# Second norm of a hybrid transformer block: four row blocks of the first gate unit multiplied before the root is known, the root applied in PSUM, five weight blocks split ahead

## The chip, the cores and the metric

The kernel runs on one core of one Trainium2 chip. Its metric is the device time of one execution in microseconds (us). Three runs of the kernel before took 2433.78, 2435.13 and 2435.26 us; their median is 2435.13 us. Engines are named as in the profile: PE multiplies matrices, PEld loads its weights, DVE and ACT do elementwise work, POOL and SP mostly issue transfers (DMAs).

## The reference, cut to what matters

One layer of a generator over 512 latent tokens of width 2048: two groups of recurrent heads, an output projection with a residual, and a SwiGLU feed-forward with a 3x3 depthwise convolution on its gate branch. All data are float32. The change lies between the output projection and the feed-forward:

```python
def rmsnorm(x, g):
    y = x * rsqrt(mean(square(x), axis=-1) + EPS)
    return y * g
...
x = x + gt1 * merge_groups(...)                  # einsum with w_out
h2 = rmsnorm(x, g_norm2) * (1 + sc2) + sh2       # the second norm
u = einsum('btd,df->btf', h2, w_up)
u_gate, u_val = split(u, 2)
g = conv3x3(u_gate) + conv_b
x = x + gt2 * ((silu(g) * u_val) @ w_down)
```

The root `rsqrt(...)` is one number per token, the scale `g_norm2 * (1 + sc2)` and the shift `sh2` are one number per row of the width. So `W^T h2` is the root times `W^T (scale * x)`, plus `W^T shift`, for all rows or for some of them.

## The kernel before, in words

Activations lie transposed: a row block is 128 of the 2048 rows of the width on the partitions, and 512 tokens along the free dimension. There are 16 row blocks (`KT`), taken in 8 pairs (`KP`). Every large product is done three times with the operands split in a high and a low part (`mm3`: high by high, low by high, high by low). ACT makes the high part by a cast (`hi_...`), DVE the low part by a subtraction (`lo_...`). The helper `mm` records every product at line 113, so the trace is read by the names of the tiles.

The output projection (`wo`) runs as four units, `n` = 0 to 3. Each unit makes four row blocks of the result in four PSUM accumulators and goes through eight weight blocks of 512 KB (`raw_wo`, split into `hi_wo` and `lo_wo`, two buffers each). After a unit, DVE adds the residual (`residual`, L1210, `x<-wo,mod,x`), POOL stores the row block to DRAM, ACT squares it (`square`, L1220), and DVE adds the squares into one tile, `sqsq` (L102), except the last two, which stay apart. During the projection DVE also works off the modulation vectors (`raw_m<-raw_m,crow`, L332, with loads of 512 KB), which give `modc[3]` (shift) and `modc[4]` (scale) for the second norm.

Then comes the second norm. `token_rstd` sums the squares over the partitions by products with a column of ones (`ps_rms`), ACT and DVE make the root (`mean_rsqrt`, L176 to L181, on four columns), and a second set of products spreads the root over the partitions (`rb_rms`). Three and seven further products, whose results nobody reads, stand before and after those (`idle_products`, named `rb_rms<-sqsq,cst` and `idle<-sqsq,cst` in the trace).

With the root, three instructions make one normed row block: DVE multiplies by scale and root (L1290, `x<-x,mod,rb_rms`), ACT adds the shift into the high part (L1291, `bqh`), DVE makes the low part (L1292, `bql`). The first gate unit (`ug`, `up_gate(0)`, 384 columns in three accumulators) multiplies all 16 row blocks in eight steps with weight blocks of 384 KB, and the first value unit (`uv`) does the same with its own weights. At the same time DVE and ACT make sums of row blocks (`token_sums`, tiles `bth`, `btl`), which the later units need: these take 512 columns with seven products for each two by two of blocks (`seven`). The convolution of the first unit (`cv`, L1384) runs on DVE during the value unit and the second gate unit, and its result (`gh`, `gl`) is what the first down unit (`dn`) multiplies with the weights `hi_d`, `lo_d`.

The order on each engine comes from a scheduler that follows the program's order and moves forward what stands under `tc.high_priority()`. Where `pinned` is set, PE keeps the program's order: it does so from the last output unit to the end of the norm. An engine executes its list strictly in order. Loads of weights go through SP's queue, in order too. A new tile pool takes the memory of a closed one and waits for its last readers.

## Time and profile before

| what | us |
|---|---|
| median of three runs | 2435.13 |
| the profiled execution | 2434.19 |
| its span, first to last instruction | 2432.0 |
| PE busy in the span | 2406.7 (99%) |
| DVE busy | 1801.9 (74%) |
| ACT busy | 1015.7 (42%) |
| last output unit's products end, about | 1063.6 |
| products of the first gate unit begin | 1071.65 |
| products of the first value unit begin | 1104.58 |
| first product of the second gate unit | 1137.22 |
| first product of the first down unit | 1177.37 |

Times within the execution are counted from the start of the span. A row of the timeline gives the start, the length, the engine, the line, the operation and, where they are equal and follow each other, their number; in square brackets stands how long the engine had been idle before it and what ended that. Instructions of one engine overlap a little, so that the distance of two starts, not the length, is what one costs in a row of equal ones. A row of the table by stretches of time gives the busy time of PE, PEld, DVE, ACT and POOL with the number of instructions, then the granted clock of PE, the busy share of the DMA engines and GB/s.

### The profile page before, as it was taken

The numbers are of one execution on the slowest core, as the hardware profiler recorded it, in microseconds if no ns is written. First come the engines' busy times: TensorE is split into PE (matmuls) and PEld (weight loads), VectorE is DVE, ScalarE is ACT, GpSimd is POOL, SyncE is SP. The second block draws the span as 40 slices with busy tenths as digits, with TensorE's granted clock in tenths as the row PEclk, the third lists the DMA queues.
The fourth block names the chain that finished last, engine by engine and source line by source line (L and its number), as shares of the span: only waits on it lengthen the run. The fifth ranks groups of instructions, "written<-read, shape, count | busy, mean of one in ns | idle before, by whom it ended". The sixth has DMA issues, their size and how long they took to land.

```text
span 2432.0 us, 38493 instructions
## 1 busy us (share of the span) xinstructions
PE 2406.7 (99%) x15334; PEld 2167.3 (89%) x15334; DVE 1801.9 (74%) x2880; ACT 1015.7 (42%) x1508; POOL 179.6 (7%) x227
## 2 busy tenths in 40 slices
PE   8999999999999999999999999999999999999998
PEld 5888899899988888888898989898989999999997
DVE  6777856645556576779987887878787878787886
ACT  5235533322223232256544444544444444444445
POOL 0000000000000000000202010101010111111022
PEclk9999999999999999999999999999999999999999
DMA  9951111233355798833646464645555555546464
GB/s 386 332 176 44 46 53 53 81 128 114 122 199 198 230 331 273 288 115 113 156 119 161 117 154 116 157 113 144 134 131 142 134 140 123 147 124 153 114 184 137
DMA packets 120902, 375.73 MB, mean 154 GB/s; under 512 B 13976, under 2 KB 14994, under 8 KB 120722
## 3 DMA queue, kind: packets, MB, share of 16 engines
q1 hardware_dynamic: 93634, 318.46, 39.3%
q0 software_dynamic: 26656, 54.03, 12.1%
q8 instruction: 120, 1.97, 0.3%
q10 hardware_dynamic: 432, 0.79, 0.1%
q14 instruction: 60, 0.49, 0.1%
HBM read 322.87 MB, written 50.35 MB: 153 GB/s over the span
## 4 chain that ended last, share of the span: by engine, by line
PE 92%; DVE 4%; DMA 2%; ACT 1%; issue 1%; SPq 0%; DVEq 0%
PE a L113 18%; PE uv L113 18%; PE ug L113 18%; PE dn L113 17%; PE ga L113 7%; PE wo L113 7%; PE po L113 2%; DVE cv L1384 1%; PE sl L113 1%; PE ps_m L113 1%; DMA raw_m<-in_w_mod 1%; PE st L113 1%; DMA raw_uv<-in_w_up 1%; PE cst L113 1%; DVE lo_d L108 0%
## 5 line engine op out<-in xcount | busy, mean ns | idle before, releaser
L113 PE MATMUL dn<-gh,lo_d 128*128 128x512 f32 x672 | 262.5, 391 | 1.1 <-DVE lo_d L108 1.1
L113 PE MATMUL dn<-gh,hi_d 128*128 128x512 f32 x672 | 261.8, 390 | 0.0
L113 PE MATMUL dn<-gl,hi_d 128*128 128x512 f32 x672 | 261.7, 389 | 0.0
L1384 DVE SCALAR_TENSOR_TENSOR cv<-pads,cwt,cv 128x512 f32<-128x512 f32 x344 | 238.9, 745 | 0.6
L1438 POOL DMA_DIRECT2D x2d<-st x160 | 140.2, 927 | 1141.5 <-ACT st L1437 1059.9
L108 DVE TENSOR_TENSOR lo_buv<-sum_uv,hi_buv 128x1024 fp32r<-128x1024 f32 x80 | 98.0, 1225 | 103.4 <-ACT hi_buv L107 103.3
L332 DVE SCALAR_TENSOR_TENSOR raw_m<-raw_m,crow 128x1024 f32<-128x1024 f32 x128 | 154.5, 1228 | 1.2 <-DMA raw_m<-in_w_mod 1.2
L113 PEld LDWEIGHTS dn<-gh,lo_d 128*128 128x128 f32 x672 | 126.1, 188 | 29.8 <-DVE lo_d L108 3.8
L113 PE MATMUL a<-hi_h,hTh 128*128 128x256 f32 x512 | 151.7, 296 | 0.5 <-ACT e L450 0.5
L113 PEld LDWEIGHTS dn<-gl,hi_d 128*128 128x128 f32 x672 | 126.2, 188 | 26.0
L113 PEld LDWEIGHTS dn<-gh,hi_d 128*128 128x128 f32 x672 | 126.2, 188 | 25.7
L113 PE MATMUL a<-lo_h,hTh 128*128 128x256 f32 x512 | 144.7, 283 | 0.0
L113 PE MATMUL a<-hi_h,hTl 128*128 128x256 f32 x512 | 144.7, 283 | 0.0
L107 ACT CAST hi_d<-raw_d 128x1024 fp32r<-128x1024 f32 x86 | 88.6, 1031 | 132.6 <-PE ug L113 70.6
L108 DVE TENSOR_TENSOR lo_d<-raw_d,hi_d 128x1024 fp32r<-128x1024 f32 x86 | 102.8, 1195 | 47.9 <-ACT hi_d L107 47.2
L113 PE MATMUL ug<-bth,hi_bug 128*128 128x256 f32 x480 | 136.8, 285 | 0.2 <-DVE t L1403 0.2
L113 PE MATMUL uv<-bql,hi_auv 128*128 128x256 f32 x480 | 135.9, 283 | 0.0
L113 PE MATMUL uv<-bqh,lo_auv 128*128 128x256 f32 x480 | 135.9, 283 | 0.0
L113 PE MATMUL uv<-bth,hi_buv 128*128 128x256 f32 x480 | 135.9, 283 | 0.0
L113 PE MATMUL uv<-btl,hi_buv 128*128 128x256 f32 x480 | 135.9, 283 | 0.0
L113 PE MATMUL uv<-bth,lo_buv 128*128 128x256 f32 x480 | 135.9, 283 | 0.0
L113 PE MATMUL ug<-bqh,lo_aug 128*128 128x256 f32 x480 | 135.9, 283 | 0.0
(432 smaller groups left out, 7267.4 us busy)
## 6 DMA issues: line engine op xcount, KB each, us to landing
raw_m<-in_w_mod SPq DMA_DIRECT2D x184, 512.0 KB, 5.0
raw_d<-in_w_down SPq DMA_DIRECT2D x82, 512.0 KB, 3.5
raw_ug<-in_w_up SPq DMA_DIRECT2D x80, 512.0 KB, 3.5
x2d<-st POOLq DMA_DIRECT2D x160, 256.0 KB, 5.4
raw_uv<-in_w_up SPq DMA_DIRECT2D x80, 512.0 KB, 5.0
raw_h<-in_w_heads SPq DMA_DIRECT2D x64, 512.0 KB, 3.5
raw_ga<-in_w_gates SPq DMA_DIRECT2D x32, 512.0 KB, 3.6
raw_wo<-in_w_out SPq DMA_DIRECT2D x32, 512.0 KB, 4.8
```

The costliest lines, as they stand in the source:

```text
L107: cast[0] = S.copy(hi, x).ins
L108: return V.tensor_tensor(out=lo, in0=x, in1=hi.bitcast(F32), op=ALU.subtract).ins
L113: ins = PE.matmul(*args, **kw)
L332: V.scalar_tensor_tensor(out=x, in0=x, scalar=1.0, in1=crow[0], op0=ALU.mult, op1=ALU.mult, accum_out=mtot[:, at : at + 1])
L1384: V.scalar_tensor_tensor(out=t3, in0=src, scalar=w, in1=t3, op0=ALU.mult, op1=ALU.add)
L1438: nc.gpsimd.dma_start(x2d[k], t, accum_op=ALU.add)
```

## The change

In the first gate unit, the row blocks 0 to 3 (weight blocks 0 and 1) are no longer multiplied as normed rows but as bare ones: the row block times its scale, split (`bare_tile`, tiles `bh`, `bl`), without root and shift. These 36 products stand on PE between the last output unit, the sums of the squares, the spread of the root and the normed products. The ten idle products are gone. When the accumulators hold the four bare row blocks, DVE multiplies each of the three in PSUM by the root (`settle`, with a copy of the root in SBUF, `r2s`), and the other twelve row blocks are added as before. The shift's share of the four row blocks is made from the weights: DVE scales the raw weights by the shift and adds them up (`shift_w`), three products with the column of ones sum that over the partitions (`ps_shift`), and ACT adds it as a bias when it moves the accumulators out (`gate_shift`).

The weight blocks 2 to 6 of the gate unit are loaded and split during the third and fourth output unit (`gate_ahead`), blocks 0 and 1 during the fourth. The last two squares are added up like the others (`apart=False`), so that `ps_rms` is four products, not twelve. The normed row blocks are made in the order 4 to 15, 0 to 3, the first of them in an order written out; the value unit takes its weight blocks in the order 2 to 7, 0, 1. The tiles of `token_sums` take the memory of the bare tiles and the weights split ahead, once the gate unit is through.

```diff
-    def unit_steps(src, name, xh, xl, accs, late=False, rates=None, queue=()):
+    def unit_steps(src, name, xh, xl, accs, kps=range(KP), queue={}):
...
-    def square(k, sums, pl, tag, sl=slice(0, T)):
+    def square(k, sums, pl, tag, sl=slice(0, T), apart=True):
...
-        if first or k >= KT - 2:
+        if first or (k >= KT - 2 and apart):
             sums.append(sq)
...
+    def gate_ahead(kp):
+        gate_w[kp] = [pre.tile([P, 2, 384], F32R, name=f"g{p}_{kp}", tag=f"{p}{kp}") for p in "hl"]
+        split(*gate_w[kp], gate_raw(kp))
+
+    def bare_tile(k):
+        sk = modc[4][:, k : k + 1]
+        for part, name in ((bh, "h"), (bl, "l")):
+            part.append(bare.tile([P, T], F32R, name=f"b{name}{k}", tag=f"{name}{k}"))
+        S.activation(bh[k], x2[k], AF.Copy, scale=sk)
+        V.scalar_tensor_tensor(out=bl[k], in0=x2[k], scalar=sk, in1=bh[k].bitcast(F32), op0=ALU.mult, op1=ALU.subtract)
+
+    def gate_product(i, kp, kk, xh, xl, start=False, stop=False):
+        wh, wl = (w[:, kk, P * i : P * i + P] for w in gate_w[kp])
+        mm3(gate_accs[i], wh, wl, xh, xl, start, stop, skip_group_check=True)
+
     for n in range(4):
         pinned[0] = n == 3
+        if n > 1:
+            for kp in ((2, 3), (4, 5, 6))[n - 2]:
+                gate_ahead(kp)
+        if n == 3:
+            assert {3, 4} <= mods_done
+            for k in range(4):
+                bare_tile(k)
         accs = unit(a["w_out"][n], f"wo{n}", yh, yl)
...
+    shift_w = bare.tile([P, 384], F32, name="shift_w")
+    for kp in range(2):
+        raw = gate_raw(kp)
+        with tc.high_priority():
+            gate_w[kp] = split_new(raw, f"ug0_{kp}", (2, 384))
+        for kk in range(2):
...
+                V.scalar_tensor_tensor(out=shift_w, in0=raw[:, kk, :], scalar=bk, in1=shift_w, op0=ALU.mult, op1=ALU.add)
+    gate_accs = [acc(f"ug0_{i}") for i in range(3)]
+    root = token_rstd(sums2, rp, "rms2")
+    for i in range(3):
+        gate_product(i, 0, 0, bh[0], bl[0], start=True)
     with tc.high_priority():
-        _, r2 = token_rstd(sums2, rp, "rms2", idle=3)
-        idle_products(acc("idle", (P, P)), sums2[0][:, 0:P], 7)
+        next(root)
+    for i in range(3):
+        gate_product(i, 0, 1, bh[1], bl[1])
+    ps = psb("ps_shift", (P, 3))
+    for i in range(3):
+        mm(ps[:, i : i + 1], shift_w[:, P * i : P * i + P], cst[:, C_ONE : C_ONE + 1], start=(i == 0), stop=(i == 2),
+           skip_group_check=True)
+    S.copy(gate_shift, ps)
+    with tc.high_priority():
+        r2 = next(root)
+        r2s = bare.tile([P, T], F32, name="r2s", tag="h0")
+        S.copy(r2s, r2)
+    for i in range(3):
+        for kk in range(2):
+            gate_product(i, 1, kk, bh[2 + kk], bl[2 + kk], stop=kk == 1)
...
+    def settle(i):
+        return V.tensor_tensor(out=gate_accs[i], in0=gate_accs[i], in1=r2s, op=ALU.mult)
+
     with tc.high_priority():
...
+        for k in (4, 5):
+            kept(weigh(k))
+            kept(upper(k))
+        for step, x in ((settle, 0), (lower, 4), (lower, 5), (settle, 1), (weigh, 6), (upper, 6), (settle, 2), (weigh, 7),
+                        (upper, 7), (lower, 6), (lower, 7)):
+            kept(step(x))
+        for k in [*range(8, KT), *range(4)]:
...
     def up_gate(q):
         if q == 0:
-            accs = unit(a["w_up3"][0], "ug0", *h2, n=3, late=True, queue=((last_square[0],), last_rsqrt))
+            for kp in range(2, KP):
+                if kp not in gate_w:
+                    gate_w[kp] = load_split(a["w_up3"][0][kp], f"ug0_{kp}", w=384, queue=normed[9])
+                for i in range(3) if kp < KP - 1 else reversed(range(3)):
+                    for kk in range(2):
+                        k = 2 * kp + kk
+                        gate_product(i, kp, kk, h2[0][k], h2[1][k], stop=k == KT - 1)
             with tc.high_priority():
-                for i, ps in enumerate(accs):
-                    S.copy(pads[:, i, 1 : ROWS + 1, 1 : GW + 1], ps.rearrange("p (r c) -> p r c", c=GW))
+                for i, ps in enumerate(gate_accs):
+                    S.activation(pads[:, i, 1 : ROWS + 1, 1 : GW + 1], ps.rearrange("p (r c) -> p r c", c=GW), AF.Identity,
+                                 bias=gate_shift[:, i : i + 1])
...
-    for _ in unit_steps(a["w_up3"][1], "uv0", *h2, accs):
+    for _ in unit_steps(a["w_up3"][1], "uv0", *h2, accs, [*range(2, KP), 0, 1], {2: normed[15], 3: normed[3]}):
```

The instruction lists of three places follow; in a row stand the line, the operation, output and inputs, and the size.

PE between the last output unit and the gate unit, before (the first row is the last product of `wo`):

```order
L113 MATMUL wo_3_8806<-yTh_7844,lo_wo_7_9055 128x512
L113 MATMUL ps_rms_9108<-cst,sqsq_8159 128x1 x4
L113 MATMUL ps_rms_9108<-cst,sqsq_9102 128x1 x4
L113 MATMUL ps_rms_9108<-cst,sqsq_9106 128x1 x4
L113 MATMUL rb_rms_9130<-sqsq_8159,cst 128x128 x3
L113 MATMUL rb_rms_9130<-cst,rs_rms_9123 128x128 x4
L113 MATMUL idle<-sqsq_8159,cst 128x128 x7
L113 MATMUL ug_0_9268<-bqh_9182,hi_ug_0_9273 128x512
```

The same place in the change, from the sums of the squares to the spread of the root (nine bare products stand ahead of these rows, 18 follow them, then the normed ones):

```order
L113 MATMUL ps_rms_9191<-cst,sqsq_8165 128x1 x4
L113 MATMUL ug_0_9179<-bh_8843,hi_ug_0_9165 128x512
L113 MATMUL ug_0_9179<-bl_8844,hi_ug_0_9165 128x512
L113 MATMUL ug_0_9179<-bh_8843,lo_ug_0_9166 128x512
L113 MATMUL ug_1_9180<-bh_8843,hi_ug_0_9165 128x512
L113 MATMUL ug_1_9180<-bl_8844,hi_ug_0_9165 128x512
L113 MATMUL ug_1_9180<-bh_8843,lo_ug_0_9166 128x512
L113 MATMUL ug_2_9181<-bh_8843,hi_ug_0_9165 128x512
L113 MATMUL ug_2_9181<-bl_8844,hi_ug_0_9165 128x512
L113 MATMUL ug_2_9181<-bh_8843,lo_ug_0_9166 128x512
L113 MATMUL ps_shift<-cst,shift_w 128x1 x3
L113 MATMUL rb_rms_9219<-cst,rs_rms_9198 128x128 x4
```

The list has nine bare products between the sum of the squares and the root's spread, where three idle products stood, and the sum is one row, not three.

DVE from the last residuals to the root, before:

```order
L1210 SCALAR_TENSOR_TENSOR x_13_9084<-wo_1_8804,mod_63,x_13_9084 128x512
L102 TENSOR_TENSOR sqsq_8159<-sqsq_8159,sqsq_9092 128x512
L1210 SCALAR_TENSOR_TENSOR x_14_9086<-wo_2_8805,mod_63,x_14_9086 128x512
L102 TENSOR_TENSOR sqsq_8159<-sqsq_8159,sqsq_9097 128x512
L1210 SCALAR_TENSOR_TENSOR x_15_9088<-wo_3_8806,mod_63,x_15_9088 128x512
L108 TENSOR_TENSOR lo_ug_0_9274<-raw_ug_0_9271,hi_ug_0_9273 128x768
L177 TENSOR_SCALAR rs_rms_9121<-ps_rms_9108 128x4
L179 SCALAR_TENSOR_TENSOR rs_rms_9122<-rs_rms_9123 128x4
L99 TENSOR_TENSOR rs_rms_9122<-rs_rms_9122,rs_rms_9121 128x4
L181 SCALAR_TENSOR_TENSOR rs_rms_9123<-rs_rms_9122,rs_rms_9123 128x4
L108 TENSOR_TENSOR lo_ug_1_9298<-raw_ug_1_9295,hi_ug_1_9297 128x768
L1290 SCALAR_TENSOR_TENSOR x_0_8149<-x_0_8149,mod_65,rb_rms_9130 128x512
```

The same place in the change:

```order
L108 TENSOR_TENSOR lo_ug_0_9166<-raw_ug_0_9163,hi_ug_0_9165 128x768
L1204 SCALAR_TENSOR_TENSOR x_12_9134<-wo_0_8855,mod_63,x_12_9134 128x512
L1204 SCALAR_TENSOR_TENSOR x_13_9136<-wo_1_8856,mod_63,x_13_9136 128x512
L102 TENSOR_TENSOR sqsq_8165<-sqsq_8165,sqsq_9144 128x512
L1204 SCALAR_TENSOR_TENSOR x_14_9138<-wo_2_8857,mod_63,x_14_9138 128x512
L102 TENSOR_TENSOR sqsq_8165<-sqsq_8165,sqsq_9149 128x512
L1204 SCALAR_TENSOR_TENSOR x_15_9140<-wo_3_8858,mod_63,x_15_9140 128x512
L102 TENSOR_TENSOR sqsq_8165<-sqsq_8165,sqsq_9154 128x512
L108 TENSOR_TENSOR lo_ug_1_9174<-raw_ug_1_9171,hi_ug_1_9173 128x768
L102 TENSOR_TENSOR sqsq_8165<-sqsq_8165,sqsq_9159 128x512
L179 TENSOR_SCALAR rs_rms_9196<-ps_rms_9191 128x4
```

The two last squares are now added to `sqsq`, and the low part of weight block 1 stands between these two additions; that of block 0 has moved ahead of the residuals.

DVE at the end of the second gate unit, where the convolution of the first unit ends (`gl` is an operand of the first down unit, `lo_d` its weights), before:

```order
L108 TENSOR_TENSOR gl_9808<-cv_9779,gh_9807 128x512
L108 TENSOR_TENSOR lo_aug_7_10219<-raw_ug_7_10215,hi_aug_7_10218 128x768
L99 TENSOR_TENSOR cv_9790<-cv_9790,uv0s_9750 128x512
L108 TENSOR_TENSOR gl_9813<-cv_9790,gh_9812 128x512
L108 TENSOR_TENSOR lo_bug_7_10226<-sum_ug_7_10217,hi_bug_7_10225 128x1024
L108 TENSOR_TENSOR lo_d_0_10288<-raw_d_0_10285,hi_d_0_10287 128x1024
L1366 TENSOR_TENSOR pads<-u_ug_10271,ug_1_9817 128x2x4x64
L96 TENSOR_TENSOR u_ug_10271<-u_ug_10271,ug_3_9819 128x512
```

The same place in the change:

```order
L1461 SCALAR_TENSOR_TENSOR cv_9815<-pads,cwt,cv_9815 128x512
L99 TENSOR_TENSOR cv_9793<-cv_9793,uv0s_9771 128x512
L1461 SCALAR_TENSOR_TENSOR cv_9815<-pads,cwt,cv_9815 128x512
L99 TENSOR_TENSOR cv_9804<-cv_9804,uv0s_9773 128x512
L108 TENSOR_TENSOR lo_bug_7_10251<-sum_ug_7_10242,hi_bug_7_10250 128x1024
L1461 SCALAR_TENSOR_TENSOR cv_9815<-pads,cwt,cv_9815 128x512
L108 TENSOR_TENSOR gl_9828<-cv_9793,gh_9827 128x512
L108 TENSOR_TENSOR gl_9833<-cv_9804,gh_9832 128x512
L99 TENSOR_TENSOR cv_9815<-cv_9815,uv0s_9775 128x512
L108 TENSOR_TENSOR lo_d_0_10313<-raw_d_0_10310,hi_d_0_10312 128x1024
L1443 TENSOR_TENSOR pads<-u_ug_10296,ug_1_9842 128x2x4x64
L108 TENSOR_TENSOR gl_9838<-cv_9815,gh_9837 128x512
```

Taps of the convolution (`cv<-pads,cwt,cv`) now stand on both sides of `lo_bug_7`, the last weights of the second gate unit, and the last `gl` stands behind the down unit's first weights.

More of the change, by code (lines that the diff above doesn't have):

```diff
@@ L132, in block_kernel @@
     mtot = keep.tile([P, 128], F32, name="mtot")
-    eps = keep.tile([P, 128], F32, name="eps")[:, 0:1]
+    few = keep.tile([P, 128], F32, name="few")
+    eps, gate_shift = few[:, 0:1], few[:, 4:7]
     modc = {n: keep.tile([P, KT], F32, name=f"mod{n}") for n in (2, 3, 4, 5)}
@@ L139, in block_kernel @@
     mod_raw = []
+    mods_done = set()
     mod_turn = [0]
@@ L231, in load_sums @@
         return plain, sums
-    def unit_steps(src, name, xh, xl, accs, late=False, rates=None, queue=()):
+    def unit_steps(src, name, xh, xl, accs, kps=range(KP), queue={}):
         n = len(accs)
-        for kp in range(KP):
-            if rates:
-                rate[0] = rates[kp]
-            wh, wl = load_split(src[kp], f"{name}_{kp}", w=P * n, queue=queue[kp] if kp < len(queue) else ())
-            if kp == 0 and late:
-                for m, (ws, xs) in enumerate(((wh, xh), (wl, xh), (wh, xl))):
-                    for k in range(2):
-                        for i in range(n):
-                            mm(accs[i], ws[:, k, P * i : P * i + P], xs[k], start=(m == 0 and k == 0), stop=False)
-                continue
-            for i in reversed(range(n)) if late and kp == KP - 1 else range(n):
+        for kp in kps:
+            wh, wl = load_split(src[kp], f"{name}_{kp}", w=P * n, queue=queue.get(kp, ()))
+            for i in range(n):
                 for kk in range(2):
@@ L250, in unit_steps, with unit @@
                     mm3(accs[i], wh[:, kk, P * i : P * i + P], wl[:, kk, P * i : P * i + P],
-                        xh[k], xl[k], k == 0, k == KT - 1)
+                        xh[k], xl[k], k == 2 * kps[0], k == 2 * kps[-1] + 1)
                 yield 1.36
-    def unit(src, name, xh, xl, n=4, late=False, rates=None, queue=()):
+    def unit(src, name, xh, xl, n=4):
         accs = [acc(f"{name}_{i}") for i in range(n)]
-        for _ in unit_steps(src, name, xh, xl, accs, late, rates, queue):
+        for _ in unit_steps(src, name, xh, xl, accs):
             pass
@@ L335, in mod_end @@
     def mod_end(region):
+        mods_done.add(region)
         o = modc[region]
@@ L1250, in block_kernel, with gate_raw @@
     sums2 = []
+    st_r = ExitStack()
+    bare, pre = (st_r.enter_context(tc.tile_pool(name=n, bufs=1, side="right")) for n in ("bare", "pre"))
+    bh, bl, gate_w = [], [], {}
+    def gate_raw(kp):
+        return load_raw(a["w_up3"][0][kp], f"ug0_{kp}", w=384)
+    def gate_ahead(kp):
[10 more added lines that the diff above has]
+        mm3(gate_accs[i], wh, wl, xh, xl, start, stop, skip_group_check=True)
     for n in range(4):
         pinned[0] = n == 3
+        if n > 1:
[5 more added lines that the diff above has]
+                bare_tile(k)
         accs = unit(a["w_out"][n], f"wo{n}", yh, yl)
@@ L1273, in block_kernel @@
               for n, b in (("mraw", 4), ("mhi", 2), ("mlo", 2), ("ahi", 2), ("alo", 2), ("msum", 2))]
-    bp = pool(ctx, "bp", waits="tile")
+    bp = {"q": pool(ctx, "bq", waits="tile")}
     fp = pool(ctx, "fp", waits="tile")
-    stp = pool(ctx, "stp", 3, waits="tile")
     def operand(j, part, what, name, shape, dtype=F32R):
-        return bp.tile(list(shape), dtype, name=name, tag=f"b{part}{what}{j}")
+        return bp[what].tile(list(shape), dtype, name=name, tag=f"b{part}{what}{j}")
     def flat(x):
@@ L1440, in block_kernel @@
     up_gate(0)
+    st_r.close()
+    bp["t"] = pool(ctx, "bt", waits="tile")
+    stp = pool(ctx, "stp", 3, waits="tile")
+    bt = [[operand(j, part, "t", f"bt{part}{j}", (P, 3, HW)) for j in range(KP)] for part in "hl"]
+    PRODUCTS = ((0, 0, bq, 0), (0, 1, bq, 2), (0, 2, bq, 1), (1, 2, bt, 2), (1, 0, bt, 1), (1, 1, bt, 0), (1, 3, bq, 3))
     st_p.close()
```

28 lines of the change are left out of this document (19 added, 9 removed).

## The prediction

> **What bounds the kernel now.** I read the page's busy table first, then the chain of waits around the second norm, then each engine's timeline there.
>
> ```profile
> PE 2406.7 (99%) x15334; PEld 2167.3 (89%) x15334; DVE 1801.9 (74%) x2880; ACT 1015.7 (42%) x1508; POOL 179.6 (7%) x227
> ```
>
> PE is never long without an instruction, so only time in which PE does something that nobody needs, or creeps, can be won. The chain shows such a place:
>
> ```profile
> 1039.95 23.81 PE wo L113 x105
> ...
> 1063.91 2.99 PE ps_rms L113 x24
> 1066.90 3.15 PE rb_rms L113 x14
> 1070.05 1.56 PE idle L113 x14
> ...
> 1071.65 32.93 PE ug L113 x144
> 1104.58 32.64 PE uv L113 x144
> ```
>
> Columns are start, length, engine, tile, count. The last output unit gives one product per 23.81/105 = 0.227 us, so another could have started at 1063.6; the gate unit starts at 1071.65. These 8.05 us hold the sum of the squares, the root and ten idle products. They are the most that this edit can win. What lies around them:
>
> ```profile
> 1020.00:1063.50 43.50, 43.50 (x194) 35.89 (x192) 26.55 (x39) 10.75 (x13) 2.70 (x5) 1.00 0.54 192
> 1071.60:1103.80 32.20, 32.17 (x143) 26.59 (x143) 32.18 (x55) 29.09 (x46) 0.00 (x0) 1.00 0.25 78
> 1103.80:1136.80 33.00, 33.00 (x147) 27.35 (x146) 32.98 (x66) 20.36 (x36) 0.00 (x0) 1.00 0.42 140
> 1136.80:1177.30 40.50, 40.50 (x338) 40.42 (x337) 37.39 (x57) 18.07 (x24) 0.00 (x0) 1.00 0.25 77
> ```
>
> These are stretches of time: last output unit, first gate unit, first value unit, second gate unit. The third busy figure is DVE: 26.55 of 43.5 us in the first, full in the second and third (32.18 of 32.20, 32.98 of 33.00), 3.1 us free in the fourth. So from the norm on DVE has just enough time, and that decides how much of a gain on PE lasts.
>
> **The gate unit's new length.** All times are of the profiled execution (2434.19 us, span 2432.0). Its 144 products stay, at 32.93/144 = 0.229 us. Between them now stand three small things.
>
> ```profile
> 1063.91 2.99 PE L113 MATMUL ps_rms<-cst,sqsq 128*128 128x1 f32 x24 [0.17 <-PE wo L113]
> 1066.76 1.63 PE L113 MATMUL rb_rms<-sqsq,cst 128*128 128x128 f32 x6
> 1068.18 1.87 PE L113 MATMUL rb_rms<-cst,rs_rms 128*128 128x128 f32 x8
> 1069.89 1.73 PE L113 MATMUL idle<-sqsq,cst 128*128 128x128 f32 x14
> ```
>
> The profile has two records for each such float32 product. The sum took 24 records from 1063.91 to 1066.76, 0.119 us each; its four products now cost 8 x 0.119 = 0.95. The three `ps_shift` products, of the same form, cost 6 x 0.119 = 0.7. The spread of the root is 8 records: 0.23 each in its own row (1.87/8), 0.12 each in the idle products behind it (1.73/14). The rows of the granted clock (last but two) tell why:
>
> ```profile
> 1064.00:1065.00 1.00, 1.00 (x10) 1.00 (x11) 0.54 (x1) 0.43 (x1) 0.18 (x2) 1.00 0.31 127
> 1066.00:1067.00 1.00, 1.00 (x8) 1.00 (x8) 0.91 (x1) 0.06 (x1) 0.00 (x0) 0.70 0.64 262
> 1068.00:1069.00 1.00, 1.00 (x6) 1.00 (x6) 0.84 (x2) 0.16 (x1) 0.00 (x0) 0.50 0.89 224
> 1069.00:1070.00 1.00, 1.00 (x7) 1.00 (x7) 0.15 (x1) 0.00 (x0) 0.00 (x0) 0.59 0.36 144
> 1070.00:1071.00 1.00, 1.00 (x11) 1.00 (x10) 0.91 (x2) 0.13 (x1) 0.00 (x0) 1.00 0.72 197
> ```
>
> After some 3 us of one-column products the clock fell to a half (0.70 over a slice: at 1066.4), and it came back at 1069.8 (0.59), 3.4 us later. In the change no stretch without wide products is longer than 2 us (below). I take the full clock, 8 x 0.12 = 0.95; the other end is 1.87, plus products of the gate unit at half speed.
>
> The Trainium skill (TensorE: Matmul & The Clock Gate, Part 1, "What's actually happening") says that the clock drops to half after an idle window of about 3.4 us, in windows that run free. Read literally it speaks against this row, where PE was busy throughout; only if one-column products count as idle does the trace agree. By that reading the new order, with 2 us at most, keeps the full clock and the sum stands; by the literal one the gate has nothing to drop for either.
>
> Now the wait ahead of the sum, the one new wait that I see on PE:
>
> ```profile
> 1063.12 0.69 DVE L102 TENSOR_TENSOR sqsq<-sqsq,sqsq 128x512 f32<-128x512 f32 x1
> 1063.79 0.75 DVE L1210 SCALAR_TENSOR_TENSOR x<-wo,mod,x 128x512 f32<-128x512 f32 x1
> ...
> 1077.36 0.95 DVE L108 TENSOR_TENSOR lo_ug<-raw_ug,hi_ug 128x768 fp32r<-128x768 f32 x1
> 1078.23 2.07 DVE L1292 SCALAR_TENSOR_TENSOR bql<-x,mod,bqh 128x512 fp32r<-128x512 f32 x3
> ```
>
> The last residual frees DVE at 1064.45 (0.66 after its start). In the new list follow the addition of the third-last square (0.65), the low part of weight block 1 (0.87, the distance of the last two rows) and the addition of the last square (0.65), whose ACT square is done at 1065.2:
>
> ```profile
> 1064.57 0.63 ACT L1220 ACTIVATE sqsq<-x 128x512 f32<-128x512 f32 x1 [0.72 <-DVE x L1210]
> ```
>
> So `sqsq` is ready at 1066.7. PE has done nine bare products by 1063.6 + 2.05 = 1065.65 and waits 1.05 us; behind that wait stand all its other products. The sum runs to 1067.65.
>
> ```profile
> 1066.94 0.26 ACT L176 ACTIVATE rs_rms<-ps_rms,eps 128x4 f32<-128x4 f32 x1 [1.01 <-PE ps_rms L113]
> ...
> 1067.86 0.16 DVE L181 SCALAR_TENSOR_TENSOR rs_rms<-rs_rms,rs_rms 128x4 f32<-128x4 f32 x1
> ...
> 1070.09 2.72 DVE L1290 SCALAR_TENSOR_TENSOR x<-x,mod,rb_rms 128x512 f32<-128x512 f32 x4 [0.95 <-PE rb_rms L113]
> ```
>
> The root takes 1.1 us from sum to last step (1066.9 to 1068.02), hence until 1068.8; PE covers it with nine bare products and the shift, until 1070.4. The spread is done at 1071.35, 18 bare products keep PE until 1075.5. In that time DVE does two normed rows (0.66 apart in the row of 1070.09), the first accumulator times the root, and two low parts: 1071.5 + 5 x 0.66 = 1074.8, just ahead of PE. `settle` is not in the trace; an addition of that size took 0.69 (row of 1063.12) and a residual out of PSUM 0.75, a gain is excluded because it is new work, and I take a distance of 0.66.
>
> From 1063.6 to the value unit: 32.93 + 0.95 + 0.7 + 0.95 + 1.05 = 36.6 against 1104.58 - 1063.6 = 41.0. **PE reaches the value unit 4.4 us earlier.**
>
> **What DVE gives back.** DVE starts its normed rows at 1071.5, 1.4 later than at 1070.09. Up to the first down unit it has lost five splits (blocks 2 to 6, 5 x 0.87 = 4.35) and gained three `settle` (2.0): it arrives 0.95 earlier, PE 4.4 earlier. DVE is thus 3.45 late against PE, with the 3.1 us free in the second gate unit to catch up. Part of that time lies here:
>
> ```profile
> 1169.43 0.69 DVE L108 TENSOR_TENSOR gl<-cv,gh 128x512 fp32r<-128x512 f32 x1 [0.69 <-ACT gh L107]
> 1170.38 1.23 DVE L108 TENSOR_TENSOR lo_bug<-sum_ug,hi_bug 128x1024 fp32r<-128x1024 f32 x1 [0.25 <-ACT hi_bug L107]
> 1173.54 1.22 DVE L108 TENSOR_TENSOR lo_d<-raw_d,hi_d 128x1024 fp32r<-128x1024 f32 x1 [1.93 <-ACT hi_d L107]
> ...
> 1183.96 1.22 DVE L108 TENSOR_TENSOR lo_d<-raw_d,hi_d 128x1024 fp32r<-128x1024 f32 x1
> ```
>
> If all of it is usable, 0.35 is given back; if none, 3.45. In the new list taps and a `gl` do fill it, but they push the down unit's evictions and seeds of the convolution back, and the next `lo_d` (here at 1183.96) stands behind those. Laying the lists of PE, ACT and DVE out with the distances of such rows I get waits of PE for `lo_d` of 1.1, 0.3 and 0.3 us in the down unit's second to fourth block. I take 1.6, near the middle. Behind the down unit DVE has free time again (74% busy over the span), and a PE that arrives earlier stays earlier.
>
> **Moved work, costed at nothing.** In the third and fourth output unit DVE gets five splits (4.8 us by 0.95), the split of block 0, four low parts (3.0) and four scalings of at most 0.75 each (3.0), about 12 us, against 17 us free in the fourth alone (43.50 - 26.55). ACT has 33 free there. The cover is real if no weight comes late:
>
> ```profile
> 1047.24 1.05 ACT L107 CAST hi_wo<-raw_wo 128x1024 fp32r<-128x1024 f32 x1 [4.38 <-PE wo L113]
> 1052.68 1.05 ACT L107 CAST hi_wo<-raw_wo 128x1024 fp32r<-128x1024 f32 x1 [4.38 <-PE wo L113]
> ```
>
> ```profile
> 1042.89 1.23 DVE L108 TENSOR_TENSOR lo_wo<-raw_wo,hi_wo 128x1024 fp32r<-128x1024 f32 x1 [3.07 <-ACT hi_wo L107]
> ...
> 1048.33 1.23 DVE L108 TENSOR_TENSOR lo_wo<-raw_wo,hi_wo 128x1024 fp32r<-128x1024 f32 x1 [1.93 <-ACT hi_wo L107]
> ```
>
> The loads there, with size and time to landing:
>
> ```profile
> raw_m<-in_w_mod SPq DMA_DIRECT2D x46, 512.0 KB, 5.0
> ...
> raw_ug<-in_w_up SPq DMA_DIRECT2D x8, 384.0 KB, 3.2
> ```
>
> ACT casts a block when PE leaves the one two before it, every 5.44 us. The low part of 1048.33 is done at 1049.56 and needed when PE starts that block, after 1052.68: 3.5 us to spare. Without that cover each us of delay costs one. On SP's queue the blocks 2 to 6 stand among the output unit's weights, 0 and 1 behind the last modulation load. The five earlier loads move 2 MB from the gate unit's time, where the DMA engines were 0.25 busy, into units where they were 0.54 and more; the bytes are the same. The sums of row blocks wait for the gate unit's end, since they take memory from it:
>
> ```profile
> 1097.12 1.98 ACT L107 CAST bth<-x 128x512 fp32r<-128x512 f32 x4
> ```
>
> They began here 7 us before the value unit; DVE has the low parts of rows 0 to 3 in their place. On POOL only the clearing of `pads` moves, behind the stores. The idle products go without cost if the clock holds. Bias instead of copy at the eviction, the late loads of the convolution's weights, and the other order of the value unit lie beside PE's 33 us of value products.
>
> **The sum.** 2434.19 - 4.4 + 1.6 = 2431.4. The median of the runs, 2435.13, lies 0.9 above the profiled execution, so 2432.3. About 0.2% (4.9 us) is what a measurement of this kernel can tell from no change; the forecast is a gain of 2.8, within that.
>
> **Rivals.** (1) DVE catches up in full: only 0.35 comes back, -4.05, 2431.1. For it the 3.1 us; against it that 1.93 of these are a wait for ACT just where the new list is dense. (2) Little lasts: DVE gives back 3.45, or the clock falls once more. One 3.4 us window at half clock would cost up to 1.7 on PE and the spread 0.9, in which case the DVE wait shrinks; either way -0.9 or so, 2434.2. The same holds if the edit doesn't do what it says because `settle` and the first low parts come late: their reserve above is 0.7 us, and three `settle` at twice the price cost 2.0 less that, 1.3. (3) Slower: in the fourth output unit DVE's scalings of the raw weights stand ahead of `lo_wo`, so DVE waits for a load. Block 1 can be issued when `lo_wo` of 1042.89 frees its buffer, at 1044.1. With 3.2 us to landing and two scalings (1.0) it delays the `lo_wo` of 1048.33 by nothing; 5.0 us, which the modulation loads take, by 1.8, within the reserve of 3.5. It decides from a landing of 6.7 us on, and the gain of 2.8 is gone at 9.5. At 12 us PE waits 5.3, 2437.6. Against it: DMA 0.54 busy there.
> **How the numbers follow.** Forecast (-1.5 to -3.5): 0.5. Rival 1: 0.2. Rival 2: 0.23. Rival 3: 0.07. The range takes in both ends of DVE's share, 4.4 in full with a run at the lower edge, and the small delays of rival 3: 2429.2 to 2436.6. Faster by over 0.2% (under 2430.3) needs rival 1 with a term mis-sized as well: 0.13. Slower by over 0.2% is most of rival 3 and what I did not see: 0.07. Within: 0.80.
>
> **What would show it.** Right: the value unit starts about 36.6 us after the last output product, one idle time of about 1 us ahead of `ps_rms`, the granted clock 1.00 throughout, waits of PE for `lo_d` of 1 to 2 us in the first down unit. Wrong: idle time of PE in the output units or ahead of the first normed products, a clock of 0.50 near the norm, no wait in the down unit, or waits that go on in the later units.

## The result and the profile after

The changed kernel takes 2416.37 us (median of 6 runs, 2414.72 to 2418.08) against 2435.44 us (6 runs of the kernel before beside it, 2433.78 to 2436.34): the ratio is 0.992, 95% interval 0.991 to 0.9931, or 19 us less. The forecast was 2432.3 us, in a range of 2429.2 to 2436.6. It was wrong, and no rival named the cause. One execution of the last kernel of experiment 5 showed about half the granted clock (0.523) and took 4521.72 us; it is left out of that kernel's figures, and every other time here is of executions at 0.996 or more.

The busy table of the page, after:

```profile
span 2415.4 us, 38457 instructions
...
PE 2387.2 (99%) x15304; PEld 2145.0 (89%) x15304; DVE 1806.2 (75%) x2893; ACT 1018.9 (42%) x1514; POOL 179.5 (7%) x227
```

PE is as full as before, with 19.5 us less to do. Only 30 short records are gone, all of them at the norm, and all that stood between the last output product and the gate unit took about 8 us before. So most of the 19.5 can only come from the same products taking less time. The chain around the norm, after (start, length, engine, tile, count):

```profile
1064.28 2.10 PE ug L113 x9
1068.26 2.20 PE ug L113 x9
1072.03 29.26 PE ug L113 x126
1101.29 32.64 PE uv L113 x144
...
1183.61 9.62 DMA x2d<-st
...
1211.36 39.36 PE uv L113 x336
```

The value unit starts 37.0 us behind the last output product (1101.29 - 1064.28); the forecast was 36.6. That step held. Counted the same way (from the end of the last output product at 1063.75) it was 40.8 before, so PE is 3.8 us ahead there. Before, the second value unit began at 1210.75, 147.0 us behind the last output product; now it begins 147.1 behind it (1211.36 - 1064.28). So the whole local gain of 3.8 us is gone by the end of the first down unit, and the 19 us do not come from the norm. The last row shows where they come from: a value unit of 336 products takes 39.36 us. Two rows of the chain of before, a gate and a value unit of that size:

```profile
1137.22 40.31 PE ug L113 x336
...
1210.75 40.31 PE uv L113 x336
```

There are 20 such units, and each is 0.8 to 1.05 us shorter. Which of the products? The view of one tile, `bth`, in the units from 1300 us on (minimum/median/maximum duration in ns), first before, then after:

```profile
L113 PE MATMUL uv<-bth,hi_buv x418: 282/283/284, 1337.6 to 2350.0; 128*128 128x256 f32 x140
L113 PE MATMUL uv<-bth,lo_buv x417: 282/283/284, 1337.9 to 2349.9; 128*128 128x256 f32 x139
```

```profile
L113 PE MATMUL uv<-bth,hi_buv x432: 276/276/286, 1336.4 to 2342.9; 128*128 128x256 f32 x144
L113 PE MATMUL uv<-bth,lo_buv x432: 276/276/279, 1336.6 to 2343.2; 128*128 128x256 f32 x144
```

Products that stream a `bt` tile became 7 ns shorter; those that stream `bq` kept their median of 283 against the weights `hi_a`, `lo_a` and came to 280 to 282 against `hi_b`, `lo_b`, where they stand behind `bt` products. The distance of two starts, averaged over the 20 units, says it more exactly: without the few distances that hold a wait, it is on `bt` 119.98 -> 114.63 ns, 2880 products, 15.4 us; on `bq` 119.98 -> 119.16 ns, 3840 products, 3.1 us. Neither the operation nor its shape changed. What changed is where the `bt` tiles lie. The diff gives them a pool of their own, opened behind the convolution's weights and `pads`, whose 12,736 bytes are no multiple of 256 (192 is left). In the memory map of the compiled programs `bth0` went from byte 159744 of a partition (a multiple of 1024) to 172480 (448 past one, 192 within 256). `bq` and the weights of these units stayed on multiples of 1024.

### The profile page after: what moved, and what is told of

It reads as the page before. It is cut to its first block, busy times and chain, and to the rows that moved or that the text cites. A ratio compares the mean times of both kernels' runs of the same rounds, so it can differ in the third digit from the quotient of the medians.

```text
span 2415.4 us, 38457 instructions
## 1 busy us (share of the span) xinstructions
PE 2387.2 (99%) x15304; PEld 2145.0 (89%) x15304; DVE 1806.2 (75%) x2893; ACT 1018.9 (42%) x1514; POOL 179.5 (7%) x227
## 4 chain that ended last, share of the span: by engine, by line
PE 92%; DVE 4%; DMA 2%; ACT 1%; issue 1%; SPq 0%; DVEq 0%; ACTq 0%
PE dn L113 18%; PE ug L113 18%; PE uv L113 18%; PE a L113 17%; PE ga L113 7%; PE wo L113 7%; PE po L113 2%; PE sl L113 1%; PE st L113 1%; DMA raw_m<-in_w_mod 1%; PE ps_m L113 1%; PE cst L113 1%; DVE ex L96 0%; DMA xl<-in_xT 0%; DMA x2d<-st 0%
## 5 line engine op out<-in xcount | busy, mean ns | idle before, releaser
L113 PE MATMUL uv<-bqh,hi_auv 128*128 128x256 f32 x480 | 135.6, 282 | 0.0
L113 PE MATMUL ug<-bql,hi_aug 128*128 128x256 f32 x480 | 135.5, 282 | 0.0
L113 PE MATMUL ug<-bqh,hi_aug 128*128 128x256 f32 x480 | 135.5, 282 | 0.0
```

The lines of the kernel that those rows point to most:

```text
L113: ins = PE.matmul(*args, **kw)
```

## The experiments

All times are medians; the kernel before ran beside each group at 2435.6 to 2435.9 us. "Distance" is that of two starts in the trace, averaged over the products of the 20 units; "offset" is an address, or a difference of two, within 256 bytes.

**1. Only the place, without the edit of the norm.** The kernel before with unused memory around `bt`:

```diff
+    gap0 = bp.tile([P, 112], F32, name="gap0", tag="gap0")
+    G.memset(gap0, 0.0)
     bt = [[operand(j, part, "t", f"bt{part}{j}", (P, 3, HW)) for j in range(KP)] for part in "hl"]
+    gap1 = bp.tile([P, 144], F32, name="gap1", tag="gap1")
+    G.memset(gap1, 0.0)
```

> The kernel before, with 448 bytes of unused memory ahead of the bt tiles and 576 behind them, so that each bt tile lies 448 bytes past a multiple of 1024 as it does in the changed kernel; nothing else moves against 1024. Theory A (the place of the bt tiles in memory sets the distance of the products that read them): distance of products on bth and btl 120 -> 114 to 115 ns, time 2419 us (2435.4 less some 16.5). Theory B (the new order around the norm, or the swapped turn of the two weight buffers, spaces the later products closer): distances stay at 120 ns, time 2435 us.

Measured: 2417.09 us, ratio 0.9924 (0.9909 to 0.9938), 18.7 us less; distance on `bt` 114.59 ns, on `bq` 119.16. Its chain:

```profile
1138.48 39.36 PE ug L113 x336
...
1211.16 39.36 PE uv L113 x336
```

448 bytes of nothing give 18.7 of the 19 us (15 to 22 by the interval). Theory A stands. The order around the norm and the turn of the weight buffers, both as before here, are out as the cause of the shorter distances.

**2. Only the edit of the norm, without the place.** The changed kernel, `bt` back on multiples of 1024:

```diff
-    cbt = fp.tile([P, 152], F32, name="cbt")[:, 0:NF]
+    cbt = fp.tile([P, 296], F32, name="cbt")[:, 0:NF]
```

> The changed kernel, with 576 bytes more in front of the bt tiles, so that they lie at multiples of 1024 again; the edit of the norm stands whole. Theory A: distances on bth and btl back at 120 ns, time 2432 to 2436 us, and what is left against the kernel before is the worth of the edit of the norm itself. Theory B: 114 to 115 ns, 2416 us as the changed kernel.

Measured: 2432.65 us (10 runs), ratio 0.9986 (0.9976 to 0.9995); all distances 119.98 ns again. The edit that the forecast was about is worth 3.2 us (1 to 6); forecast 2.8. What PE waited for, from 1060 us to 1300:

```profile
PE uv L113 <- DVE lo_buv L108: 1.2, 1, 1.2
PE dn L113 <- DVE lo_d L108: 1.1, 1, 1.1
PE ps_rms L113 <- issue: 0.9, 1, 0.9
```

In the profiled execution PE is 3.8 us ahead at the first value unit, has lost 1.3 of it by the end of the first down unit and 3.0 by the end of the second value unit. That leaves less than the medians show; executions of the kernel before differ too, in two places that experiment 7 shows.

**3. Which places are good.** Two scans within the changed kernel: `bt` tiles 3136 bytes apart, so that each has another offset, then 3104 apart (4 floats more asked for, which the allocation rounds up to 32 bytes) with the down units' weights at 16 offsets in turn, `off` in floats.

```diff
-    bt = [[operand(j, part, "t", f"bt{part}{j}", (P, 3, HW)) for j in range(KP)] for part in "hl"]
+    bt = [[bp["t"].tile([P, 3 * HW + 16], F32R, name=f"bt{part}{j}", tag=f"b{part}t{j}")[:, 0 : 3 * HW].rearrange("p (a b) -> p a b", b=HW)
+           for j in range(KP)] for part in "hl"]
...
+            if name[0] == "d":
+                off = 4 * (turn[0] % 16)
+                turn[0] += 1
...
```

> The changed kernel, with the sixteen bt tiles 3136 instead of 3072 bytes apart, so that each lies at another one of the sixteen multiples of 64 within 1024. Theory A: the distance differs by tile, 120 ns where the offset is 0 and 114 at 448, and the rest tells which offsets are bad. A variant of it (only a multiple of 1024 or 512 is bad): one or two of the sixteen at 120, time 2416 to 2418 us. Theory B: all sixteen at 114 to 115 ns.

> The changed kernel, as a finer scan: the bt tiles lie 32 bytes further on from one to the next (eight offsets within 256), and the split weights of the down units lie at 16 offsets of 16 bytes within 256, in turn, against moving tiles at 0. The scan in steps of 64 gave 120 ns at 0, 118 at 64, 119 at 128, 114.6 at 192, with a period of 256. Theory A2 (distance of moving tile and weights, within 256): 120 at 0 and a smooth or stepped fall around 192, perhaps a better place at 160 or 224; for the down products of 512 columns (227 ns at 0) a spread of some ns over the 16 offsets, 229 to 232 where the weights lie 192 on. Rival (only multiples of 64 matter): offsets 32 apart pair up in equal values. Time between 2416 and 2430 us.

Measured distances in ns by the offset of the moving tile from the weights (256 columns, `bt`; 512 columns, down units):

| offset | 0 | 32 | 64 | 96 | 128 | 160 | 192 | 224 | 240 |
|---|---|---|---|---|---|---|---|---|---|
| 256 columns, first scan | 119.9 | | 118.0 | | 119.0 | | 114.6 | | |
| 256 columns, finer scan | 120.0 | 118.1 | 118.0 | 120.0 | 118.9 | 117.4 | 114.6 | 118.2 | |
| 512 columns | 227.8 | 233.3 | 229.6 | 233.3 | 232.3 | 233.8 | 233.1 | 232.9 | 227.0 |

The first scan has 16 offsets within 1024 and repeats every 256: 114.6 to 115.2 at 192, 448, 704 and 960 alike, 120 at 0, 256, 512 and 768. The change hit the best of eight places by chance. The values for 256 columns are averages over `bth` and `btl`, which differ by up to 3.4 ns (at 32: 119.2 and 115.8). For 512 columns it is the other way round: an equal place (227.8), 16 (227.6) and 240 are the good ones, and most others cost 4 to 6 ns, 64 only 2. So the second scan as a whole took 2434.64 us, outside its 2416 to 2430, and the first 2425.84 (one execution each). Steps of 32 differ, so the rival that only 64 matters is out.

**4. Address, or distance from the weights?** First the split weights moved by 448 bytes as well, then a mirror: the kernel before with 64 bytes ahead of the weights `hi_a`, `lo_a` and 192 behind them.

```diff
-    wts[:] = [pool(ctx, n, b, waits="tile")
-              for n, b in (("mraw", 4), ("mhi", 2), ("mlo", 2), ("ahi", 2), ("alo", 2), ("msum", 2))]
...
+    wts[:] = [pool(ctx, "mraw", 4, waits="tile")]
+    gap("gap0", 112)
+    wts += [pool(ctx, n, b, waits="tile") for n, b in (("mhi", 2), ("mlo", 2), ("ahi", 2), ("alo", 2), ("msum", 2))]
+    gap("gap1", 144)
```

> The changed kernel, with the split weights (hi, lo) 448 bytes later as well, bq at multiples of 1024 as before and bt 448 past one. Theory A1 (the address of the moving tile alone counts): bt products stay at 114 to 115 ns, bq products at 119 to 120, time 2416 us. Theory A2 (what counts is the distance between the moving tile's address and that of the weights being loaded at the same time): bt products back to 120 ns, bq products down to 114; four of seven products are bq, so against a kernel with all at 120 (2433) some 22 us less, 2411 us. Theory B: all as in the changed kernel, 2416 us.

> The kernel before, with 64 bytes of unused memory ahead of the weights hi_a, lo_a of the later units and 192 behind them; all moving tiles stay at 0 within 256, all other weights too. It is the mirror of moving bt: three of the seven products of a two by two of blocks (bqh, bql against hi_a, lo_a) then have a distance of moving tile and weights of -64, which is 192 within 256. Theory A2 (that distance counts): these products go from 120 to 113 to 116 ns, the others stay, 2418 to 2421 us. Theory A1 (the moving tile's own address counts, the weights' doesn't): all stay at 120, 2435.5 us.

Measured: 2427.39 us, ratio 0.9963 (0.995 to 0.9976), for the first. `bt`, where the changed kernel has it but with weights at the same offset, is back at 120.08 ns; `bq`, which did not move, went to 117.76. The expected 114 was missed: `bq` lies 448 bytes below the weights here, which is 64 within 256, and for 64 the scan has 118.0. The tile views of the changed kernel with moved weights show it in the medians:

```profile
L113 PE MATMUL uv<-bth,hi_buv x426: 277/283/290, 1335.9 to 2348.5; 128*128 128x256 f32 x142
L113 PE MATMUL uv<-bqh,hi_auv x428: 276/280/283, 1333.9 to 2350.0; 128*128 128x256 f32 x143
...
L113 PE MATMUL dn<-gh,lo_d x498: 392/394/394, 1300.0 to 2201.5; 128*128 128x512 f32 x166
```

So the moving tile's address alone does not set it; its distance from the weights agrees with all of these: theory A1 is out. The time fits: `bq` 8.5 us less than in experiment 2, the down products (392 to 394 ns here against 389) some 3 us more. The mirror agrees in kind, 2429.56 us, ratio 0.9976 (0.9967 to 0.9986), with the three products against `hi_a`, `lo_a` moved and the rest at 120. It misses in size: 117.5 to 118.2 ns instead of 113 to 116, so 6 us instead of 15. At the same distance of 192 the products can thus be 114 or 118 ns apart.

**5. Everything at the good distance.** The changed kernel with `bq` at 192 as well; then the same with the first pair (`bqh0`, `bql0`) left at 0; then, instead, `hi_a` and `lo_a` moved by 64.

```diff
-    bq = [[operand(j, part, "q", f"bq{part}{j}", (P, 4, HW)) for j in range(KP)] for part in "hl"]
+    bq = [[operand(0, part, "q", f"bq{part}0", (P, 4, HW))] for part in "hl"]
+    G.memset(bp["q"].tile([P, 112], F32, name="gap0"), 0.0)
+    for part, b in zip("hl", bq):
+        b.extend(operand(j, part, "q", f"bq{part}{j}", (P, 4, HW)) for j in range(1, KP))
...
```

> The changed kernel, with 448 bytes ahead of the bq tiles, so that bq as well as bt lies at 192 within 256 while the weights stay at 0. Theory A2: the bq products of the later units (some 3800) go from 119.8 to 114.6 ns, as the bt products did: 20 us less, minus up to 2 us for the bq products of 512 columns in the first units, 2397 us. Rival (at this spacing something else feeds PE too slowly, the splits on DVE or the loads): waits of PE for lo_bug or lo_buv appear and less than half is left, 2407 us or more. Rival (only the place of bt counts): 2416 us.

> The changed kernel, with all bq and bt tiles at 192 within 256 but for the first pair of row blocks (bqh0, bql0), which stays at 0; weights at 0. With everything at 192 the products of a unit kept one of two distances throughout, 113.4 or 117.7 ns, while bt products that came behind products at offset 0 took 113.4 in nearly every block. Theory C (two steady patterns at 192, which one is set by the products at the unit's start): the first 18 products of a unit at 120, all that follow at 113 to 114, so 20 units x some 300 x 4 ns less than with everything at 192, 2390 to 2396 us. Rival (one pattern per unit at random, or set by something else): as with everything at 192, 2413 us.

> The changed kernel with the same shift of hi_a and lo_a: now six of the seven products have the distance 192, the seventh (the fourth part of bq against hi_b, lo_b) keeps 0 and stands once in every block of weights, and the down products of 512 columns keep 0 too. Theories A2 and C together: 36 of 42 products of a block at 113.4 ns, six at 120, a few ns at the passage, in every block: 150 to 220 ns less for each of 160 blocks than with all at 120 (2432.65), 2398 to 2408 us. Rival (the pattern of 117.7 ns takes over once bq and bt both lie at 192): 2413 us, as with everything at 192.

Measured: 2413.15 (ratio 0.9911, 0.9895 to 0.9928), **2402.61** (0.9857, 0.9841 to 0.9874) and 2412.39 us (0.9905, 0.9886 to 0.9925). The first gave 3 us against the changed kernel instead of 20. PE waits for neither `lo_bug` nor `lo_buv` there, so the rival of a slow feed is out, and the distances themselves are longer. The chains of the first and of the second kernel, whole value units:

```profile
1208.86 39.57 PE uv L113 x336
...
2300.24 39.57 PE uv L113 x336
```

```profile
2291.40 38.25 PE uv L113 x336
```

39.57/336 is 117.8 ns, 38.25/336 is 113.8. With everything at 192 each value unit ran from its first product to its last at 117 to 119 ns, while gate units fell to 113.4 in 6 of 10 cases and then kept it. With 18 products at offset 0 first, all units but four settled at 113.4; in three of the four the distance changed to 118 at the second block of weights and stayed there. That two steady patterns exist is shown; that what goes ahead decides which one a unit gets is only supported. The size was missed (2390 to 2396 was expected), and two kernels speak against products at offset 0 as the whole rule: in the mirror of experiment 4 such products stand ahead in every block of weights, and those behind them keep 118; with `hi_a` and `lo_a` moved in the changed kernel, stretches of 113 and 118 ns took turns (2398 to 2408 was expected). What sets the pattern stays open. The version with the first pair at 0 beats the changed kernel by 14 us and the kernel before by 33.

**6. Who takes the local gain back: the stores.** Experiment 2's kernel with more buffers for the evicted sums of the first down unit. By the edit there are six instead of four: three of `st` and the tiles 0, 1 and 3; the forecast below counts seven.

```diff
-                    t = ytile(15 if q else 0, name) if i == 3 else stp.tile([P, T], F32, name=name, tag="st")
+                    y = {3: 15 if q else 0} if q or blk % 2 == 0 else {0: 1, 1: 3, 3: 0}
+                    t = ytile(y[i], name) if i in y else stp.tile([P, T], F32, name=name, tag="st")
```

> The changed kernel with the bt tiles back at multiples of 1024, and in the first down unit seven instead of four buffers in turn for the evicted sums (st). In that unit ACT waits up to 1.4 us for an adding store to leave a buffer, and the cast of the next weights (hi_d) stands behind it, then lo_d, then PE. Theory E (the stores, not DVE's own work, take the gain back there): ACT's waits for x2d<-st and PE's wait for lo_d (1.1 us) in that unit go, 2431.5 us. Theory D (DVE's work): the waits for lo_d stay, 2432.65 us.

In experiment 2's kernel PE waits for `lo_d` until 1201.3. The rows of ACT and DVE that lead up to it (the timeline; in brackets the idle time ahead and what ended it):

```profile
1192.03 0.69 ACT L1514 ACTIVATE st<-dn,mod 128x512 f32<-128x512 f32 x1 [1.87 <-DMA x2d<-st]
1192.92 0.69 ACT L1514 ACTIVATE st<-dn,mod 128x512 f32<-128x512 f32 x1 [0.20 <-DMA x2d<-st]
1193.51 0.61 ACT L107 CAST hi_d<-raw_d 128x512 fp32r<-128x512 f32 x1
```

```profile
1194.15 0.69 DVE L108 TENSOR_TENSOR lo_d<-raw_d,hi_d 128x512 fp32r<-128x512 f32 x1 [1.09 <-ACT hi_d L107]
1194.76 5.38 DVE L1461 SCALAR_TENSOR_TENSOR cv<-pads,cwt,cv 128x512 f32<-128x512 f32 x8
1200.06 1.22 DVE L108 TENSOR_TENSOR lo_d<-raw_d,hi_d 128x1024 fp32r<-128x1024 f32 x1
```

ACT cannot write an evicted sum before the store of an earlier one has left its buffer. The cast `hi_d` stands behind that, DVE is idle for 1.09 us until the cast is done, and eight taps later its next `lo_d` comes 1.1 us too late for PE. (ACT's wait of 1.4 us, named above, lies at 1200.55, too late to cause this one.)

Measured with the buffers: 2432.35 us, ratio 0.9986 (0.9977 to 0.9996), no difference that can be told from experiment 2. But ACT's waits of 1.87 and 0.20 and PE's wait for `lo_d` in that unit are gone, and PE loses 0.1 us there instead of 1.3; by the end of the second value unit it has lost 1.3 instead of 3.0. What PE still waits for, up to 1300 us, and a row of ACT:

```profile
PE uv L113 <- DVE lo_buv L108: 1.0, 1, 1.0
PE ps_rms L113 <- issue: 0.9, 1, 0.9
```

```profile
1203.40 0.69 ACT L1515 ACTIVATE st<-dn,mod 128x512 f32<-128x512 f32 x1 [3.52 <-DMA x2d<-st]
```

ACT's waits for stores did not go, as theory E expected; they came later, the longest here. Behind it stand a cast, 2.48 us of idle time of DVE and then work of DVE without a gap up to the `lo_buv` for which PE waits. Theory E holds for the place, not for the total.

**7. Who takes it back: DVE.** Two of the nine taps of the first unit's convolution left out, in the kernel before (the control) and in experiment 2's kernel:

```diff
-            for tap in range(9):
+            for tap in range(9 if q else 7):
```

> The kernel before, with two of the nine taps of the first unit's convolution left out (six instructions on DVE, some 4 us of its time between the first value unit and the first down unit). It is the control: PE waits for DVE nowhere there, so both theories expect no change, 2435 us.

> The changed kernel with the bt tiles back at multiples of 1024 (2432.65 us), and the same two taps left out. There PE reached the value unit 3.8 us earlier than in the kernel before and lost 3 of it by the end of the second value unit, with waits for lo_d and lo_buv. Theory D (DVE, which has the same work and less time, takes it back, as the prediction said): with 4 us less on DVE the waits go, PE keeps 3 to 4 us at the third gate unit, 2429.5 to 2431 us. Rival (the loads of that stretch, or ACT, take it back): waits and time as without the edit, 2432.5 us.

Measured: the control 2436.51 us, ratio 1.0002 (0.9993 to 1.0011); the other 2431.55 us, ratio 0.9983 (0.9974 to 0.9992). Against experiment 2 that is 1.1 us less, between the two theories' times; the intervals overlap. In the profile PE keeps all it has won through the first three blocks of the down unit, then loses 0.9 there and 0.6 in the value unit: 1.5 instead of 3.0. The wait for `lo_buv` falls to 0.3 and a wait for `lo_d` of 1.2 remains. So DVE's work has a share and the stores have a share. The two were not removed together, and the exact split stays open.

The control contradicts its own premise that PE waits for DVE nowhere there. First a row of its ACT, then PE's wait behind it, then ACT's row in experiment 2's kernel:

```profile
1220.48 0.69 ACT L1437 ACTIVATE st<-dn,mod 128x512 f32<-128x512 f32 x1 [2.96 <-DMA x2d<-st]
...
1226.34 0.39 PE L113 MATMUL uv<-bth,lo_buv 128*128 128x256 f32 x1 [0.80 <-DVE lo_buv L108]
```

```profile
1216.67 0.69 ACT L1514 ACTIVATE st<-dn,mod 128x512 f32<-128x512 f32 x1 [2.85 <-DMA x2d<-st]
```

In both kernels ACT waits about 2.9 us for a store, then casts `hi_auv`; DVE is idle until that cast is done and then brings `lo_buv` too late. PE loses 1.3 us by it in the second value unit of the control, 1.4 in the mirror of experiment 4, and nothing in the profiled execution of the kernel before, all three without the edit of the norm. So the 1.7 us that experiment 2's kernel loses in that unit cannot be put down to the edit alone: a part of them depends on when the stores end, and how often it happens no run here tells.

The control shows one thing more, in the granted clock (last but two) at the norm:

```profile
1066.00:1067.00 1.00, 1.00 (x9) 1.00 (x8) 0.52 (x1) 0.45 (x1) 0.01 (x1) 0.70 0.44 184
1070.00:1071.00 1.00, 1.00 (x7) 1.00 (x7) 0.15 (x1) 0.00 (x0) 0.00 (x0) 0.50 0.00 0
1073.00:1074.00 1.00, 1.00 (x8) 0.96 (x8) 1.00 (x3) 1.00 (x3) 0.00 (x0) 0.88 0.00 0
```

Here the half clock lasted from 1066.4 (0.70) to 1073.2 (0.88), 6.8 us, twice as long as in the profiled execution of the kernel before, and the gate unit began 1.35 us later behind the sum. The forecast took the 3.4 us of the one profiled execution as the rule. That it can be twice as long, and the wait behind the stores, may be why the medians give the edit more than the pair of profiles does: the profiled execution of the kernel before had the short fall and not the wait.

## Why the prediction was wrong

**The step that failed is "Moved work, costed at nothing".** It lists the `bt` tiles: "The sums of row blocks wait for the gate unit's end, since they take memory from it." I costed the time of that move and never the place. A new address was in the diff and was worth 16 us (2432.65 to 2416.37) to 19 us (experiment 1), some six times the forecast gain. By the profiled executions, most of what lies between the two figures is lost again in the changed kernel's first down unit (below). The closing sentence "a PE that arrives earlier stays earlier" has the same hole: it takes the later units' products as fixed, at 40.31 us a unit, and they were not. The range and the chances failed with it, since every case was built on the norm alone.

**The norm's own terms, one by one.** PE after the last output product, in the changed kernel:

```profile
1067.24 1.02 PE L113 MATMUL ps_rms<-cst,sqsq 128*128 128x1 f32 x8 [0.86 <-issue]
1068.12 0.48 PE L113 MATMUL ug<-bh,hi_ug 128*128 128x512 f32 x1
...
1070.30 0.72 PE L113 MATMUL ps_shift<-cst,shift_w 128*128 128x1 f32 x6
1070.89 1.14 PE L113 MATMUL rb_rms<-cst,rs_rms 128*128 128x128 f32 x8
1071.78 0.48 PE L113 MATMUL ug<-bh,hi_ug 128*128 128x512 f32 x1
```

- Wait ahead of the sum: 0.86, forecast 1.05. Sum 0.88 (1067.24 to 1068.12), forecast 0.95. Shift 0.59, forecast 0.7. Spread 0.89, forecast 0.95.
- The 144 wide products take 33.8 us (2.10 and 2.18 for the two groups of nine, 29.51 from 1071.78 to 1101.29), where I took 32.93 from before: 0.9 more. It is the same cause with the other sign: the tiles of the bare rows and the weights split ahead lie 224 and 32 bytes from their partners by the memory map; these products are 233 ns apart, those at 0 227.
- Sum: 37.0 against 36.6. Right, partly because the small terms came out 0.4 us short and the products 0.9 long.

**Clock.** Right for the norm: it was 1.00 in every slice of the changed kernel there. By the Trainium skill (TensorE: Matmul & The Clock Gate, Part 1) an idle window halves it; as in the prediction, only the reading by which one-column products count as idle is left, and even so the window was not idle throughout: in experiment 7's control the clock fell 2.1 us behind the last output product (1064.3 to 1066.4). The 1.7 us without wide products in the changed kernel (1066.38 to 1068.12) did not bring it down; what share of a window is enough no run here settles. I did not foresee that the clock would fall in the first down unit, behind a wait of PE of 2.2 us (0.93 in the rows below).

**What is given back.** Forecast 1.6 as waits of PE for `lo_d` in the first down unit. (The three waits that I laid out add up to 1.7.) In experiment 2's kernel, to which the forecast applies, 1.3 was lost there, and 1.7 more in the second value unit, which I had excluded and of which a part comes without the edit too (experiment 7). In the changed kernel it is worse: the second gate unit is 0.95 us shorter, PE waits 2.8 us in the first down unit, and 3.4 us at half clock follow. In all 4.9 us are lost there: PE entered it 4.8 us ahead of the kernel before and leaves it 0.1 behind. The stretches of the second gate unit and of the down unit in the changed kernel, then the down unit before, then PE's waits in the changed kernel from 1060 us to 1300:

```profile
1133.70:1171.00 37.30, 37.30 (x320) 37.26 (x319) 37.30 (x57) 17.64 (x21) 0.00 (x0) 1.00 0.23 72
1186.00:1211.00 25.00, 22.80 (x93) 18.09 (x92) 21.16 (x33) 12.46 (x18) 7.83 (x9) 0.93 1.04 213
```

```profile
1177.30:1210.60 33.30, 33.09 (x147) 27.04 (x147) 31.58 (x49) 20.05 (x29) 10.54 (x12) 1.00 0.82 181
```

```profile
PE dn L113 <- DVE lo_d L108: 2.8, 2, 2.2
PE ps_rms L113 <- issue: 0.9, 1, 0.9
```

The mechanism was only half right. DVE's shortage is real (experiment 7; the third busy figure is full in the first row), but I never counted the DMA engines in that stretch: they are at 1.04 in the second row (last but one) and were at 0.82 over the whole unit before, and ACT's buffers come free when the stores are through (experiment 6). That the full engines are what makes the stores slow was not tested.

**The rivals.** Rival 1 (DVE catches up in full) did not happen: 1.3 us came back in the first down unit alone, not 0.35. Rival 2 (little lasts) describes the profiled pair without the shift of `bt`, by another path than I gave. Rival 3 did not happen: PE waits for nothing in the output units.

**The sum.** The edit alone, forecast 2432.3, measured 2432.65. That it agrees so well is partly luck: PE reached the value unit 3.8 us earlier, not 4.4, more was given back behind it than I summed, and the kernel before can lose more, at the norm and in the second value unit, than in the execution I read.

## What to carry to other kernels

A diff that opens, moves or resizes a pool changes addresses, so compare the memory maps of both programs before costing the moved work at nothing; where PE is 99% busy with small products, a few ns a product can outweigh every stall (here 5 ns on 2880 products, 15 us). When a forecast is made for one place of a program, ask what sets the pace of the other 95%. And look for the gain of an edit in the first later stretch where another resource is full, here the DMA engines at 1.04, not only where the edit's own engines are busy.

## What the runs showed of the hardware

- Float32 products of 256 columns start 113.4 to 120 ns apart, depending on the distance within 256 bytes between the moving tile and the weights: on the average of the scan 120.0 at 0 and 96, 114.6 at 192, and 117 to 119 elsewhere. With 512 columns 0, 16 and 240 are good (227 to 228) and most others cost 4 to 6 ns. The Trainium skill (TensorE: Matmul & The Clock Gate, "Wait — 56ns, not 53.3ns?") gives N/2.4 plus about 2.5 ns for back-to-back products; here, where each product also loads weights of its own (as many rows of PEld as of PE), no stretch of products came below 113.4, which is 6.7 ns above 256/2.4, and the usual 120 is 13.3 above.
- At the same distance of 192 there are two steady patterns, 113.4 and 117.7 ns, that can last for hundreds of products and change at a disturbance. What the two streams, weights and moving tile, do to each other was not seen in any record; a conflict of their reads is a guess.
- The half clock at the norm, with the same instructions there, lasted 3.4 us in the profiled execution of the kernel before and 6.8 us in that of experiment 7's control.
